# One inference step of a two-layer hybrid decoder on one core: the same operations in another order and on other engines

## The chip, the core and the metric

The kernel runs on one core of one Trainium2 chip. A core has a matrix engine (TensorE, PE in the profile; its weight loads are shown apart as PEld), three elementwise engines (VectorE = DVE, ScalarE = ACT, GpSimd = POOL) and SyncE (SP), which in this kernel issues every DMA. The metric is the time of the device in microseconds (us); lower is better.

## What is computed

There are 512 prompt tokens and 8 sequences with one new token each, handled together as T = 520 columns. Each of the two layers normalises x, multiplies by W_in, runs three mixers and adds the result of W_out to x:

```
h = rmsnorm(x) @ w_in                       # 1024 -> 3072 + 24 gates
A: GLU -> causal depthwise conv (31 taps) -> LayerNorm -> swish -> pointwise
B: trailing means over 2/4/8/16 tokens minus the token, one small product per group
C: attention, 8 query heads, 2 key/value heads: compressed blocks + selected
   blocks (top 8 of 64 rows) + window of 256, mixed by per-head sigmoid gates
x = x + concat(A * silu(zA), B * silu(zB), C * silu(zC)) @ w_out
```

The 8 sequences carry caches of 512 rows each; two of the three caches lie in pages that a page table names. New cache rows and states are outputs too.

## The kernel before, in words

The program is first written down as a list (class Plan): every engine instruction is an op, and ops that must stay together on one engine form a burst; an op alone or a burst is a *unit*. There are 3309 units, numbered as the program text makes them. `plan.place` then takes the units in the sequence of the string TUNE["order"], gives the buffers their slots in that sequence, and `emit` issues them so (line 352 is the one line that issues everything, which is why nearly every row of the profile has L352). Each engine runs its own units strictly in that sequence; across engines only data and buffers order them. A second string, TUNE["engines"], has one letter for each of the 756 elementwise ops that may run on one of several engines (v, s, g for VectorE, ScalarE, GpSimd). So the order on all five queues is written out by hand, number by number.

The large products are those of `product` (line 744): 1024 input rows in 8 chunks of 128 and 128 output columns; x and the weights are split in two fp32r parts each, and a chunk is one burst of 6 matmuls (high x high, high x low, low x high, for two halves of 260 tokens). `fetch` (592) loads the weights of one product as two halves of 256 KB, chunks 0-3 and 4-7, and `split` (724) makes the high and the low part of each half with two elementwise ops. A product holds two of the eight PSUM banks until `evac` (758) has read it.

`evac` multiplies by rb, the reciprocal norm of each token. `scale(c)` (765) makes the high and the low part of piece c of x and its square, and `sums` (689) adds the squares up by four small products in four 32-column strips of PE; `spread` (695) needs the sums of all 8 pieces, computes the reciprocal root by eleven ops on VectorE, stores it to a DRAM tile (rs) and loads it back broadcast (rb). So products can run before rb is there, but none can leave PSUM.

Small products come in several tile forms, told in the profile by rows * columns of the weights: 128\*128 (all large products and the transposes), 128\*64, 128\*32, 64\*128 (the attention scores), 64\*32 and 32\*32.

`constants` (625) also has 24 warm-up products (`warm`, 629-633), which give nothing that is used:

```
ve.memset(mean_w, 1.0 / 256.0)
warm = plan.bank("warm", "t")
for n in range(WARM // 2):
    with plan.burst():
        for k in range(2):
            te.matmul(warm[:, :128], mean_w, mean_w, start=True, stop=True)
```

Every fp32 product that is not a transpose is two matmul instructions on the chip, so the warm-up is 48 of them. `cmp_pages` (912) loads 32 pages of the compressed cache in a layer, each with a read of the page number first; `compress` (878) needs them. `decode` (1256) attends for the 8 sequences, in two groups of four.

Of the kernel before, what the change touches and what calls it, by code (L numbers as in the profile page):

```python
# [189 lines left out]
class Plan:  # L190
# [135 lines left out]
    def emit(self, tc, ctx):  # L326
# [60 lines left out]
        "vvvvgvvsssssvssgsvvggvggsvsvvssvvsgvvssvsvggsvvvgvgssgsggvvvgvsgsgsgvvggvvvsvvvvvssvsvsvsgggsvvvsvsgvgvsvgvgvssv"  # L387
        "vvsgsgsvssgvvsggsvgvsgsvsvggsvsggsvvggvggggvvssgvsssvsvsvggvvsgsgvggvvgvvgsssssggggssssvssssssvgvvggvvsvsvsgsgvv"
        "vsvvsvgsvvgvggssvvssvsvvvsvgvggggsgsvvgggggsvgvgvsssgvssvsssssvssssvsssgggvvvggsvgvvvvgvgsssssvvssvvsvvsgvvggsgg"
        "ggvggvvgvgsvvvvgsgsvvvsvgvsvsgvgsgsvsvsvsvggsvsgssggssvsvvvgvvgvgvggsvvsssvsvsssvssvgvvsssggggggvgvvvgsgsvvgssvg"  # L390
        "vsvgvsvvgsvssggvvsvgvvgvvggvsvvvvsvgvgvssvggsvvvsvssvgvsgvggvgsvggsgsgsgvgggvsggggvvvssgsvsvvsvsvsgggsgggvggvggs"
        "gsggssggssssvgsssvsvssvsgggsgvvsggvggvggvsggvssvsgvsgggssssvssvsvvvsssgvvggvggsgvvsssgggvgvgvsssssssssvsvvsvvsss"
        "sgvgvgvgvgvgvvvggvssvvvvssgvsvsvvsggvsgggvvsgsggvvsgsvgvsgggsggvsgggsgsgsvsvsvsvggvv"
    ),
    "order": (
# [1147 lines left out]
```

## Time and profile before

| | us |
|---|---|
| median of 3 runs | 624.89 (624.70 to 625.42) |
| the profiled execution, whole | 623.73 |
| its span, first to last instruction | 622.0 |

| engine | busy us | share of the span |
|---|---|---|
| PE | 606.4 | 97% |
| PEld | 536.7 | 86% |
| DVE | 433.7 | 70% |
| ACT | 259.7 | 42% |
| POOL | 226.2 | 36% |

Times in the views count from the first instruction of the span. In a list in order of time a row is: start, duration, engine, line, operation, out<-in, rows * columns of the weights and shape, and how many instructions were merged; in brackets the idle time before, and what ended it. Matmuls overlap, so the cost of a group is read from its start to the start of the next one, not from its duration.

### The profile page before, as it was taken

How to read it: one execution, taken by the hardware profiler on the slowest of the kernel's cores; microseconds unless marked ns; L12 is line 12 of the kernel's file. 1: busy time of each engine (PE TensorE's matmuls, PEld its weight loads, DVE VectorE, ACT ScalarE, POOL GpSimd, SP SyncE). 2: the span in 40 equal slices, each digit the busy share in tenths (PEclk: the TensorE clock that was granted, in tenths of full speed). 3: DMA queues.
4: the chain of work that ended last, by engine and by line, in shares of the span. 5: the costliest groups of instructions: out<-in, count | busy, mean ns of one | idle time of the engine just before them, and what ended most of it. 6: DMA issues, size and time to landing. Idle time of an engine off the chain costs nothing.

```text
span 622.0 us, 15002 instructions
## 1 busy us (share of the span) xinstructions
PE 606.4 (97%) x5526; PEld 536.7 (86%) x5526; DVE 433.7 (70%) x1222; ACT 259.7 (42%) x731; POOL 226.2 (36%) x250
## 2 busy tenths in 40 slices
PE   6999999999999999999999999999999999999997
PEld 5999998898868788579999999999985968677997
DVE  6535879966778697965465498887677678688221
ACT  4102125656683395431221132237575769543100
POOL 2123225442414363341522242556443535144700
PEclk9999999999999999999999999999999999999999
DMA  8755444322652346887546234342246135788622
GB/s 267 217 166 180 152 124 146 115 76 73 136 122 65 104 125 220 268 252 228 185 143 194 85 113 160 94 124 62 77 79 155 37 95 140 185 255 252 208 77 95
DMA packets 89130, 90.98 MB, mean 146 GB/s; under 512 B 25858, under 2 KB 59746, under 8 KB 88930
## 3 DMA queue, kind: packets, MB, share of 16 engines
q1 hardware_dynamic: 89058, 90.04, 48.9%
q8 instruction: 43, 0.70, 0.5%
q14 instruction: 29, 0.24, 0.1%
HBM read 75.32 MB, written 14.67 MB: 145 GB/s over the span
## 4 chain that ended last, share of the span: by engine, by line
PE 84%; DVE 6%; SPq 5%; DMA 3%; issue 2%; ACT 1%; ACTq 0%; DVEq 0%
PE banks L352 84%; DVE t L352 4%; SPq L352 3%; DVE small L352 2%; DMA t<-in_win 2%; SPq L616 1%; ACT t L352 1%; DMA t<-in_x 1%; DMA t<-in_cmp 0%; DVE keep L352 0%; ACTq L352 0%; DVEq L352 0%
## 5 line engine op out<-in xcount | busy, mean ns | idle before, releaser
L352 PE MATMUL banks<-t,t 128*128 128x260 f32 (+5 forms) x3960 | 490.0, 302 | 1.9 <-DVE t L352 0.8
L352 PEld LDWEIGHTS banks<-t,t 128*128 128x128 f32 (+3 forms) x3960 | 434.2, 178 | 32.8 <-issue 25.1
L352 POOL TENSOR_TENSOR t<-t,t 128x512 fp32r<-128x512 f32 (+4 forms) x84 | 111.4, 1332 | 129.2 <-PE banks L352 55.7
L352 ACT ACTIVATE t<-t 128x512 fp32r<-128x512 f32 (+4 forms) x130 | 78.5, 613 | 155.1 <-DVE t L352 56.8
L352 ACT ACTIVATE t<-t,small 128x384 f32<-128x384 f32 (+4 forms) x185 | 99.2, 552 | 16.2 <-DVE small L352 15.9
L352 PE MATMUL banks<-keep,t 128*128 128x128 f32 (+7 forms) x698 | 87.2, 311 | 1.9 <-DVE t L352 1.1
L352 DVE TENSOR_TENSOR t<-t,t 128x512 fp32r<-128x512 f32 (+3 forms) x92 | 71.0, 782 | 22.0 <-PE banks L352 16.0
L352 PEld LDWEIGHTS banks<-keep,t 128*128 128x128 f32 (+2 forms) x698 | 66.5, 161 | 22.1 <-issue 12.5
L352 DVE TENSOR_TENSOR t<-banks,t 128x520 f32<-128x520 f32 (+1 forms) x54 | 37.2, 693 | 63.8 <-PE banks L352 51.2
L352 DVE CUSTOM_DVE_ANT_0 t<-banks,keep,small 128x384 f32<-128x384 f32 (+3 forms) x128 | 64.3, 528 | 16.2 <-PE banks L352 16.0
L352 POOL TENSOR_SCALAR t<-t 128x512 fp32r<-128x512 f32 (+2 forms) x49 | 34.6, 707 | 88.3 <-PE banks L352 48.5
L352 ACT ACTIVATE t<-banks 128x512 f32<-128x512 f32 (+3 forms) x72 | 36.6, 525 | 62.1 <-PE banks L352 45.7
L352 PE MATMUL banks<-t,keep 128*32 128x130 f32 (+7 forms) x688 | 41.2, 306 | 6.7 <-DVE keep L352 4.8
L352 PEld LDWEIGHTS banks<-t,keep 128*32 128x32 f32 (+3 forms) x688 | 23.2, 116 | 20.5 <-DVE keep L352 5.0
L352 POOL TENSOR_SCALAR t<-t,small 128x384 f32<-128x384 f32 (+3 forms) x50 | 32.9, 671 | 21.2 <-DVE small L352 15.4
L352 ACT ACTIVATE small<-small 128x32 f32<-128x32 f32 (+3 forms) x76 | 23.5, 310 | 27.5 <-DVE small L352 27.4
L352 DVE COPY t<-banks 128x512 f32<-128x512 f32 (+2 forms) x37 | 21.5, 589 | 11.2 <-PE banks L352 7.3
L352 DVE SCALAR_TENSOR_TENSOR t<-t,t 128x520 f32<-128x520 f32 (+2 forms) x32 | 27.8, 873 | 1.3 <-ACT t L352 1.1
L352 POOL TENSOR_TENSOR t<-t,keep 128x520 f32<-128x520 f32 (+1 forms) x11 | 14.2, 1296 | 33.5 <-DVE t L352 20.4
L352 POOL TENSOR_TENSOR t<-t 128x520 f32<-128x520 f32 (+1 forms) x12 | 12.8, 1068 | 33.2 <-DVE t L352 13.9
L352 ACT ACTIVATION_READ_ACCUMULATOR t<-t,small 128x1 f32 x132 | 24.7, 187 | 0.0
L352 DVE SCALAR_TENSOR_TENSOR small<-small 128x130 f32<-128x130 f32 (+3 forms) x80 | 23.5, 296 | 1.5
(81 smaller groups left out, 358.1 us busy)
## 6 DMA issues: line engine op xcount, KB each, us to landing
t<-in_w_in SPq DMA_DIRECT2D x96, 256.0 KB
t<-in_cmp SPq DMA_DIRECT2D x64, 128.0 KB
t<-in_slc SPq DMA_DIRECT2D x64, 128.0 KB
t<-in_w_out SPq DMA_DIRECT2D x32, 256.0 KB
t<-in_x SPq DMA_DIRECT2D x16, 260.0 KB
t<-in_win SPq DMA_DIRECT2D x16, 256.0 KB
out_win<-t SPq DMA_DIRECT2D x16, 256.0 KB
t<-glu SPq DMA_DIRECT2D x12, 264.0 KB
```

The source lines that it names most:

```text
L352: fn(*[real(v) for v in o.a], **{k: real(v) for k, v in o.k.items()})
L616: pages[n] = tc.nc.sync.value_load(pt.real(plan)[0:1, n:n + 1], min_val=0, max_val=n_phys - 1)
```

## The change

Nothing is computed differently; the two strings are replaced. The letters go from v 274, s 251, g 231 to v 265, s 273, g 218. The order string is new in all its lines. The diff, cut to its beginning and end:

```diff
@@ -384,155 +384,155 @@
     "engines": (
-        "vvvvgvvsssssvssgsvvggvggsvsvvssvvsgvvssvsvggsvvvgvgssgsggvvvgvsgsgsgvvggvvvsvvvvvssvsvsvsgggsvvvsvsgvgvsvgvgvssv"
...
+        "sgvssssssgsgssssvgsvsvvvsvggvgsvvsgssvgvssggsvvvvgvsgvgvsgvvggvgsvssvsvgvvvsvgggvssvggvssgvgsvgvsvssgvvsvgvsvssg"
...
     ),
     "order": (
-        "78 16 35 0 36 15 27 33 17 79 2 3 4 18 34 37 80 19 39 81 84 22 40 5 6 21 115 38 82 43 57 47 20 44 48 7 41 85 59 "
-        "23 42 51 86 141 307 52 138 134 55 56 139 83 45 117 143 136 53 118 63 46 137 60 58 49 64 140 65 66 309 133 116 "
-        "145 67 68 69 87 121 8 369 61 50 144 310 54 70 9 122 119 25 10 123 71 88 72 11 73 308 74 75 311 142 76 120 124 62 "
...
-        "3270 3271 3016 3272 3285 3273 3238 3257 3286 3287 3239 3288 3289 3240 3274 3290 3291 "
+        "2 3 16 15 4 5 6 7 115 33 17 35 18 369 117 8 9 39 41 10 11 0 27 12 19 34 307 371 118 23 20 37 13 21 14 121 309 38 "
+        "36 79 40 51 47 45 22 122 78 43 144 49 42 123 372 308 55 46 375 142 61 376 377 310 50 348 378 63 313 80 124 53 82 "
+        "314 132 145 315 370 59 44 48 52 81 56 136 60 64 316 65 66 148 138 139 116 141 57 150 83 84 311 140 151 67 312 "
+        "373 54 85 58 68 86 69 87 70 221 71 119 374 317 120 72 73 74 318 88 75 76 89 25 90 319 549 379 143 77 133 380 137 "
+        "381 350 550 131 62 125 382 91 152 320 218 431 351 126 92 93 127 321 128 354 322 432 94 323 129 147 182 153 235 "
+        "383 183 355 324 154 237 95 134 356 435 433 184 96 97 325 98 326 99 327 349 216 434 155 100 101 436 149 102 437 "
...
+        "3272 3285 3238 3307 3286 3287 3273 2565 3288 3289 3239 3240 3290 3274 3308 3291 "
     ),
```

What the numbers say, read against the numbering of the units:

- Units 3 to 14 are the warm-up. Before, they stand in nine groups of 4 or 8 instructions among the first products and sums; after, all twelve stand ahead of everything else on PE. Unit 2, the memset that they read, is the first on VectorE after; before, it stood behind two ops on x.
- The first large product on PE before is k0 (units 84, ...) behind the sums of piece 0 and 8 instructions of warm-up; after, it is chunk 0 of v0 (121) directly behind the warm-up, then the sums of pieces 0 and 1. Then come 10 more chunks, out of v0, k2 and k1, then the sums of pieces 2 to 7 side by side, and then the rest of the four products k0, k1, k2, v0. All four are finished on PE before any other product begins (v1, 354 and on).
- On SP before: halves of k0, v0 and then page loads mixed with the second halves; after: x piece 0, then first halves of v0, k2 and k1 among the other pieces of x, both halves of k0, and the second half of k1 after the first page; the weights v1, q0 also stand ahead of most pages of the second group. The last of layer 0's compressed pages is the 63rd DMA before and the 71st after.
- On VectorE after, the first op on the finished sums (in `spread`) stands ahead of the low parts of k0 and k1's second halves and of pieces 5 and 6 of x.
- Changes of the tile form from one PE instruction to the next, counted along the two order strings: 186 before, 160 after.

## Rows read from the trace of the kernel before

**Rows 1.** the page: span, busy time of each engine, granted clock in 40 slices.

```profile
span 622.0 us, 15002 instructions
...
PE 606.4 (97%) x5526; PEld 536.7 (86%) x5526; DVE 433.7 (70%) x1222; ACT 259.7 (42%) x731; POOL 226.2 (36%) x250
...
PEclk9999999999999999999999999999999999999999
```

**Rows 2.** the chain in order of time: start, duration, what.

```profile
5.78 6.09 DMA t<-in_x
...
117.84 123.40 PE banks L352 x1126
...
276.82 259.20 PE banks L352 x2385
...
564.41 53.73 PE banks L352 x489
```

**Rows 3.** TensorE in order of time, the first 36 us.

```profile
4.82 0.66 PE L352 MATMUL banks<-t,keep 128*32 128x130 f32 x8 [4.82 <-DVE keep L352]
5.41 2.08 PE L352 MATMUL banks<-keep 128*128 128x128 f32 x8
7.14 1.94 PE L352 MATMUL banks<-t,t 128*128 128x260 f32 x6
9.02 0.66 PE L352 MATMUL banks<-t,keep 128*32 128x130 f32 x8
9.61 1.75 PE L352 MATMUL banks<-keep 128*128 128x128 f32 x8
11.28 0.65 PE L352 MATMUL banks<-t,keep 128*32 128x130 f32 x16
...
12.33 1.68 PE L352 MATMUL banks<-t,t 128*128 128x260 f32 x12
13.94 1.09 PE L352 MATMUL banks<-t,keep 128*32 128x130 f32 x32
...
16.50 1.05 PE L352 MATMUL banks<-keep 128*128 128x128 f32 x8
17.31 0.97 PE L352 MATMUL banks<-t,t 128*128 128x260 f32 x6
```

**Rows 4.** all engines in order of time, first 25 us; [idle before, what ended it].

```profile
0.74 1.28 ACT L352 ACT_TABLE_LOAD   x1 [0.74 <-PEq L1535]
...
3.35 0.63 ACT L352 ACTIVATE t<-t 128x512 fp32r<-128x512 f32 x1 [1.32 <-DMA t<-in_w_in]
...
4.03 0.70 DVE L352 TENSOR_TENSOR t<-t 128x520 f32<-128x520 f32 x1 [4.03 <-DMA t<-in_x]
...
5.11 0.17 DVE L352 MEMSET keep<- 128x128 f32 x1
...
23.02 0.66 SPq L352 DMA_DIRECT2D rs<-small  x1
```

**Rows 5.** busy time (and pieces) of PE, PEld, DVE, ACT, POOL; clock, DMA, by stretch.

```profile
22.00:34.00 12.00, 10.34 (x89) 9.86 (x88) 4.52 (x10) 2.54 (x4) 3.15 (x3) 1.00 0.74 232
34.00:50.00 16.00, 15.54 (x130) 15.36 (x128) 3.95 (x12) 0.00 (x0) 2.51 (x2) 1.00 0.47 143
```

**Rows 6.** who waited for whom: us in total, times, longest.

```profile
PEld banks L352 <- issue: 44.0, 131, 0.8
```

**Rows 7.** weight loads in order of time, 92 to 97 us.

```profile
95.04 0.25 PEld L352 LDWEIGHTS banks<-small 128*32 128x32 f32 x8
95.49 1.60 PEld L352 LDWEIGHTS banks<-t,t 128*128 128x128 f32 x13 [0.20 <-issue]
```

**Rows 8.** weight loads by form: names, operands, count, busy us, mean ns, idle.

```profile
L352 PEld LDWEIGHTS banks<-t,keep 128*32 128x32 f32 x512 | 12.9, 110 | 16.9 <-DVE keep L352 5.0 <-POOL t L352 3.3 <-issue 2.6
```

**Rows 9.** all engines in order of time, 22 to 36 us.

```profile
26.09 0.36 SPq L352 DMA_DIRECT2D t<-rs  x1
...
29.73 1.30 DVE L352 TENSOR_TENSOR t<-banks,t 128x520 f32<-128x520 f32 x2 [5.78 <-DMA t<-rs]
```

More of the change, by code (lines that the diff above doesn't have):

```diff
@@ L386 @@
     "engines": (
-        "vvvvgvvsssssvssgsvvggvggsvsvvssvvsgvvssvsvggsvvvgvgssgsggvvvgvsgsgsgvvggvvvsvvvvvssvsvsvsgggsvvvsvsgvgvsvgvgvssv"
[L388 to L393, printed above, removed]
+        "sgvssssssgsgssssvgsvsvvvsvggvgsvvsgssvgvssggsvvvvgvsgvgvsgvvggvgsvssvsvgvvvsvgggvssvggvssgvgsvgvsvssgvvsvgvsvssg"
+        "vgsvsvgvssvvgsggsvsvsvsgsgsvggsvsgvssgsvsgsssvsgsvssvsvvgggvvggvggggggvgggvvsgsvsssvgssvssssvsvgvsgvgvgvsvgvggvs"
+        "gvssgssggssgvvsssssssvssvssvgggsgsvssvggvvssvgssssvssgssssvssvvssssvsssgvgvvggvsvvgggggsvvsssvvvssssssvgggggvgvv"
+        "gsvgvvvvsgsvsvsgsvvvgvsgsvsggvsvvvvggggvgvsvgvsvgvgsggssssvvgggvgvvvvggssvsssvvgvvsgvgvsssgggsvgvvsvvvsvsvvgvggs"
+        "gsgvvsvvgggssgsvsvgvggsvgvgvvsvvgsgggsvssvvvsgsvggsgvgggvgsvsvvvvgvgsvsgvgsvgvssgggsvssgvvsvsvsvgggsgsgvvgvsgsgv"
+        "gssvsvssggsvssssssvsssssvvgsvvvvvvvvsgvvgvgsvvsgvvgvvgsssssssssvsvssssgggsggvgvgggvvvvsgsvvssssggsvsvsvvssvsvsss"
+        "ssggvvggvsvvggvgvsgssvvssvsvvsssssvgvsgsggvsvvgsgvgvggggsvsggvsgvvsgsvvvggsggvvvsvvg"
     ),
     "order": (
[140 rows of a table removed]
[140 rows of a table added]
     ),
```

269 rows, old and new, of the table TUNE are left out of this document.

## The prediction

> **What bounds the kernel now.** I read the page first, then the chain of waits, then TensorE's own list in order of time, and last the stretches in which TensorE has holes. [...] The chain confirms that PE sets the end and shows where it does so without a break [rows 2]: 123.40 us of nothing but PE from 117.84, and 259.20 us from 276.82. In these two stretches no other engine and no DMA matters, and an order can save there only what PE itself loses between two instructions. PE is without work for 622.0 - 606.4 = 15.6 us. Of these, 4.8 lie ahead of its first instruction [rows 3]. The list and the stretches of the first 50 us [rows 3, 5] show 12.00 - 10.34 = 1.66 and 16.00 - 15.54 = 0.46 more. Of the remaining 8.7, 3.9 are the tail, the last evacuation and its store (the last PE stretch of the chain ends at 564.41 + 53.73 = 618.1 [rows 2]); 4.8 are short waits, by the breaks in the chain mostly around the two decode steps.
>
> Busy is not the same as useful, though. The 48 warm-up instructions give nothing, and they are busy time. And the first needed product took far longer than the later ones. So the first 50 us hold more to be won than the holes show, and I price them apart.
>
> **Part 1: the start (warm-up first, x and four first halves first).** What PE spends before 50 us on anything but needed work at its later pace:
>
> - 4.82 until its first instruction.
> - The warm-up. Two groups of 8 take 7.14 - 5.41 = 1.73 and 11.28 - 9.61 = 1.67, 0.21 an instruction; a group of 8 later takes 17.31 - 16.50 = 0.81, 0.10 an instruction [rows 3]. With the other 32 at 0.10 this is 1.73 + 1.67 + 3.2 = 6.6.
> - The first chunk of k0 takes 9.02 - 7.14 = 1.88; two chunks later take 13.94 - 12.33 = 1.61, 0.80 each [rows 3]. Lost: 1.1.
> - Holes: 1.66 + 0.46 = 2.1 [rows 5].
>
> Together 14.6. After the change, the memset that the warm-up reads no longer stands behind an op on x (before: VectorE waited until 4.03 for x, and the memset came at 5.11); the other engines begin at 0.74 [rows 4], so I put the first warm-up instruction at 1.0. All 48 in a row: at 0.10 they take 4.9, at 0.21 they take 10.2. I take 20 at the slow pace, since in the run of before the pace was slow until about 11 us with holes between, and 28 at the fast one: 4.2 + 2.8 = 7.0. So the first needed product can start at 8.0. Are its operands there? A first half of weights was there 2.6 us after the first issue, at 3.35, and x at 4.03, issued after it [rows 4]; v0's half is now the third DMA, so I put it one transfer later than x had, near 5. The split (an op of 0.63 and one of 0.70) and x's two parts end near 6.5. That is before 8.0: the warm-up covers it. After that I allow 2.0 us of holes, as before. 8.0 + 2.0 = 10.0 against 14.6: **a gain of 4.6.** Bounds: with the fast pace and no hole 5.9 against 14.6, a gain of 8.7; with the slow pace and 5 us of holes 1.0 + 10.2 + 5.0 = 16.2, a loss of 1.6.
>
> The cover of the holes is thin, and it is the norm. Before, from the last sum of squares (13.94 + 1.09 = 15.0) VectorE's chain runs to the store at 23.02, the load back is issued at 26.09, and the first evacuation starts at 29.73 [rows 3, 4, 9]: 14.7 in all. After, eleven chunks (8.8) and two sums (0.5; 1.09 / 4 = 0.27 each) stand ahead of sums 2 to 7 (1.6): the last sum is at 8.0 + 10.9 = 18.9. Among the eleven ops of the chain VectorE now has five others instead of two, three more at 0.7, so the evacuation comes at 18.9 + 14.7 + 2.1 = 35.7. Until then PE can live on four products of 8 chunks, 25.6, and eight sums, 2.2: to 35.8. They just meet, with 0.1 us to spare. What sits ahead of the last sum is piece 7 of x: before, the eleventh large transfer landed at 5.78 + 6.09 = 11.87 [rows 2]; it now is the twelfth, one step of (11.87 - 3.35) / 10 = 0.85 later, 12.7. Behind it on ScalarE stand its scaling, its square and three more ops of about 0.7 before the square of piece 6, so the sums could run from 16.2; PE wants them at 17.3. On SP the store of rs stands ahead of the gate weights, and GpSimd waits for these before it makes the low parts of v1 and q0; rs would be stored at 18.9 + 8.0 + 2.1 = 29.0, the gate weights land some 3 us later, and v1's low part is there at 34, ahead of 35.8. I see nothing that must be late, and little that is early; that is what the 2.0 us of holes are for.
>
> **Part 2: tile forms side by side.** 26 of 186 changes of form go. What one costs: in the list of weight loads, eight loads of the 128\*32 form follow each other to 95.29, and the load of the 128\*128 form that follows starts at 95.49, 0.20 later, with nothing named that it waited for ("issue") [rows 7]. A load of that narrow form takes 0.11 itself [rows 8], which would be hidden in a run of one form; so about 0.1 is lost for good. The list of waits has 44.0 us of such "issue" in 131 pieces, 0.34 each [rows 6]; some of that lies under matmuls that still run. I take 0.1: 26 x 0.1 = **2.6**. Bounds: 0 (all hidden) and 26 x 0.34 = 8.8. [...]
>
> **Part 3: the letters and everything else.** 22 ops more for ScalarE (busy 259.7), 9 fewer for VectorE (433.7), 13 fewer for GpSimd (226.2) [rows 1]: some 0.7 us each, all on engines with at least 188 us to spare, hidden by the PE stretches of rows 2. If that cover were gone, it would show as new short waits. Before, the waits outside the start and the tail are 4.8; I leave them as they are: **0**, with bounds of -4.8 (all go) and +4.8 (they double). The loads of the pages end later in the queue (71st instead of 63rd DMA), at 2 us later by my count of issues; the second group of the compression also comes later on PE, so I cost this at nothing.
>
> **Sum.** 4.6 + 2.6 + 0 = 7.2. The profiled execution took 623.73 (span 622.0 and 1.7 around it): 616.5. The median of the runs is 1.16 above that execution, so I give 617.7.
>
> **The rivals.**
>
> *The norm comes too late (the other side).* The first op on the sums now stands on VectorE ahead of the low parts of k0, k1 and of pieces 5 and 6; it waits for the last sum, and while it waits nobody makes those parts. If piece 7 or a square is late, the sums, the low parts and rb are all late by the same amount, PE runs out of the four products, and banks cannot be freed. PE then stands from 35.8 on. It decides when rb comes more than 7.2 us after that, at 43 or later; at 46 the time is 617.7 + 10.2 = 627.9. For it: the in-order queues, the thin margin, the three more ops within the chain. Against it: piece 7 would have to land 7 us later than I count. Chance 0.14.
>
> *The start gives nothing.* The loads feed PE no faster than before, and only the forms pay: 624.9 - 2.6 = 622.3. For it: the DMA share in 22 to 34 us is 0.74 already [rows 5]. Against: the warm-up alone, moved into dead time, is worth more than this. Chance 0.10; half of that with the forms worth nothing as well, so 624.9.
>
> *The changes of form cost the whole wait.* 0.34 each: 4.6 + 8.8 = 13.4, 611.5. For it: the 44.0 us [rows 6]. Against: PE is 97% busy, so most of that wait lies under matmuls. Chance 0.12.
>
> *The warm-up is wasted.* Products just after a hole run at half pace, as the first chunk did (1.88 against 0.80 [rows 3]), although the page shows the upper level throughout. If PE stands between the warm-up and the first products, five chunks at 1.9 instead of 0.8 cost 5.5: 623.2. Against it: the operands are there at 6.5, before the warm-up ends. [...] No row of this run shows the granted clock fall. Chance 0.08.
>
> **How the numbers follow.** My forecast, 614 to 621.5, has 0.56; the rivals 0.14, 0.10, 0.12 and 0.08. The range of 8 in 10 leaves out the far part of the cheap end and the far part of the late norm: 611.0 to 624.5. A measurement here can tell about 0.2% (1.25 us) from no change. Slower by more: 0.14. Within 0.2%: 0.08, from the cases in which the start and forms both give little or the warm-up is wasted. Faster: 0.78.
>
> **What would show it right or wrong.** Right: warm-up instructions on PE from about 1 us on, the first 128x260 product near 8, no PE hole of over 1 us before 50, the first evacuation near 35.7 and PE not waiting for it; the sum of "issue" waits of PEld down by some 26 pieces; PE busy near 602, less than before by the forms and the slow chunk. Wrong: a hole on PE between 30 and 45 that ends with the load of rs or with an op of VectorE; a first product later than 11; decode waits grown by more than 3 us; a PE that stays as long as before from 117 us on, with the same price for each change of form.

## The result: 618.2 us, and the profile after

The changed kernel takes 618.23 us (median of 4 runs, 617.68 to 618.48) against 624.80 of the kernel before in the same session: ratio 0.9893, interval 0.9876 to 0.991. I had said 617.7, in a range of 611.0 to 624.5, with 0.78 for faster. The profiled execution took 618.43 against my 616.5 for it, so the gain between the two profiled executions is 5.3 us, where my sum was 7.2; between the medians it is 6.6.

The page of the kernel after, its lines that answer to [rows 1]: TensorE (PE) is idle for 616.7 - 605.0 = 11.7 us instead of 15.6, the granted clock reads 1.00 in all slices (what its record holds of the first microseconds stands in the last section). ScalarE has 22 instructions more, VectorE 9 and GpSimd 13 fewer.

```profile
span 616.7 us, 14975 instructions
...
PE 605.0 (98%) x5526; PEld 538.7 (87%) x5526; DVE 434.6 (70%) x1213; ACT 267.5 (43%) x753; POOL 212.1 (34%) x237
...
PEclk9999999999999999999999999999999999999999
```

PE in order of time, the first 36 us, answering to [rows 3] (start, duration, product, count; in brackets the idle time before and what ended it):

```profile
1.06 7.73 PE L352 MATMUL banks<-keep 128*128 128x128 f32 x48 [1.06 <-DVE keep L352]
8.55 0.96 PE L352 MATMUL banks<-t,t 128*128 128x260 f32 x6
...
17.40 1.54 PE L352 MATMUL banks<-t,keep 128*32 128x130 f32 x48
...
34.45 0.98 PE L352 MATMUL banks<-t,t 128*128 128x260 f32 x6 [0.24 <-DVE t L352]
```

The warm-up now fills dead time, the first needed chunk starts at 8.55 (I had said 8.0) and takes 0.96 instead of 1.94, the sums of squares end at 17.40 + 1.54 = 18.9 (said: 18.9), and no hole before 50 us is longer than 0.24. The memset that the warm-up reads stands at 0.84 instead of 5.11 [rows 4]. The end of the norm, VectorE in order of time, answering to [rows 9]: the first evacuation comes at 33.70, 2 us ahead of what I counted.

```profile
33.70 1.91 DVE L352 TENSOR_TENSOR t<-banks,t 128x520 f32<-128x520 f32 x3 [5.89 <-DMA t<-rs]
```

The same stretches as [rows 5], and the sum of "issue" waits of the weight loads that answers to [rows 6]:

```profile
22.00:34.00 12.00, 12.00 (x103) 12.00 (x101) 5.90 (x13) 0.00 (x0) 3.77 (x4) 1.00 0.55 154
34.00:50.00 16.00, 15.76 (x136) 15.01 (x135) 9.82 (x25) 3.75 (x6) 4.09 (x4) 1.00 0.69 214
```

```profile
PEld banks L352 <- issue: 33.3, 100, 0.9
```

Both stretches are now full (12.00 of 12.00, 15.76 of 16.00), and the issue waits fell by 10.7 us in 31 pieces. But the chain of waits, beside [rows 2], shows what else came in: in layer 1 the norm's store and load of rs stand in the chain. In the last decode stage the window's load does. That one is not new: it stood in the chain before, in a part that [rows 2] leaves out:

```profile
536.66 4.90 DMA t<-in_win
541.69 8.37 PE banks L352 x66
```

The kernel after:

```profile
108.90 148.56 PE banks L352 x1355
...
321.14 2.58 DMA rs<-small
323.80 5.95 DMA t<-rs
...
330.59 162.26 PE banks L352 x1549
...
532.82 3.97 DMA t<-in_win
```

In PE's list these are three holes that the kernel before did not have in this size (before, its longest after 50 us is 0.86, and its wait for the window at 541.69 is 0.65):

```profile
94.08 0.44 PE L352 MATMUL banks<-t,keep 128*32 128x136 f32 x8 [1.21 <-ACT t L352]
```

```profile
330.59 1.97 PE L352 MATMUL banks<-t,t 128*128 128x260 f32 x14 [1.29 <-DVE t L352]
```

```profile
536.17 1.07 PE L352 MATMUL banks<-t,keep 128*32 128x256 f32 x3 [1.10 <-DMA t<-in_win]
```

To see the balance I cut PE's time in each trace into pieces that add up: from the start of each instruction to the start of the next, with holes of over 0.15 us taken apart. Products of the decode stages are all that `decode` issues, its transposes too; narrow are the forms other than 128\*128.

| us | before | after | difference |
|---|---|---|---|
| ahead of the first instruction | 4.82 | 1.06 | -3.76 |
| warm-up | 6.58 | 7.49 | +0.91 |
| holes up to 50 us | 2.15 | 0.24 | -1.91 |
| holes after 50 us | 4.57 | 6.04 | +1.47 |
| narrow (tiled) products without the decode stages | 108.85 | 104.32 | -4.53 |
| full products and transposes | 469.96 | 469.37 | -0.59 |
| products of the decode stages | 20.92 | 24.03 | +3.11 |
| from the last start to the end | 4.11 | 4.11 | 0 |
| span | 621.96 | 616.66 | -5.30 |

The start gave 3.76 - 0.91 + 1.91 = 4.8, and 1.5 more that stand in the rows of products (the slow first chunk, 1.1, and the slow first sums, 0.4, both at the slow pace): 6.3 in all. The rest of these rows, 4.53 + 0.59 - 1.5 = 3.6, I put down to the forms; it is a remainder and no measurement, and it has in it, with the other sign, the transposes outside the decode stages, which take 1.5 longer. And 3.11 + 1.47 = 4.6 was given back in the decode stages and in new holes. By the middle of the kernel the lead was whole: the first sum of layer 1 starts at 319.33 before and at 312.59 after, 6.7 earlier, with as many instructions of PE ahead of it (2799 and 2803); the end is 5.3 earlier.

### The profile page after: what moved, and what is told of

Its sections match the earlier page's. It is cut to its first block, busy times and chain, and to the rows that moved or that the text cites. A ratio compares the mean times of both kernels' runs of the same rounds, so it can differ in the third digit from the quotient of the medians.

```text
span 616.7 us, 14975 instructions
## 1 busy us (share of the span) xinstructions
PE 605.0 (98%) x5526; PEld 538.7 (87%) x5526; DVE 434.6 (70%) x1213; ACT 267.5 (43%) x753; POOL 212.1 (34%) x237
## 4 chain that ended last, share of the span: by engine, by line
PE 84%; DVE 8%; DMA 5%; ACT 1%; issue 1%; SPq 1%; DVEq 0%; ACTq 0%
PE banks L352 84%; DVE t L352 5%; DVE small L352 2%; DMA t<-rs 2%; DMA out_pool_s<-small 1%; ACT t L352 1%; SPq L352 1%; DMA t<-in_cmp_w 1%; DMA t<-in_win 1%; DMA rs<-small 0%; ACT small L352 0%; DVE keep L352 0%; SPq L616 0%; DVEq L352 0%; ACTq L352 0%
## 5 line engine op out<-in xcount | busy, mean ns | idle before, releaser
L352 POOL TENSOR_TENSOR t<-t,t 128x512 fp32r<-128x512 f32 (+3 forms) x79 | 103.6, 1319 | 132.1 <-ACT t L352 33.9
L352 ACT ACTIVATE t<-t 128x512 fp32r<-128x512 f32 (+5 forms) x123 | 73.6, 612 | 161.5 <-DVE t L352 68.3
L352 PE MATMUL banks<-keep,t 128*128 128x128 f32 (+8 forms) x698 | 86.1, 311 | 1.1 <-DVE t L352 0.8
L352 DVE TENSOR_TENSOR t<-t,t 128x512 fp32r<-128x512 f32 (+5 forms) x97 | 70.1, 733 | 21.8 <-PE banks L352 8.0
L352 PEld LDWEIGHTS banks<-keep,t 64*128 64x128 f32 (+3 forms) x698 | 66.1, 161 | 21.3 <-issue 7.3
L352 POOL TENSOR_SCALAR t<-t 128x512 fp32r<-128x512 f32 (+3 forms) x57 | 38.3, 675 | 125.4 <-DMA t<-in_w_in 46.7
L352 DVE CUSTOM_DVE_ANT_0 t<-banks,keep,small 128x384 f32<-128x384 f32 (+3 forms) x128 | 64.2, 529 | 11.5 <-PE banks L352 10.7
L352 POOL TENSOR_TENSOR t<-t 128x520 f32<-128x520 f32 (+3 forms) x14 | 16.6, 1189 | 40.1 <-PE banks L352 21.1
L352 ACT ACTIVATE t<-t,keep 128x520 fp32r<-128x520 f32 (+2 forms) x21 | 17.0, 818 | 28.7 <-DVE t L352 26.0
L352 DVE CAST t<-t 128x512 fp32r<-128x512 f32 x32 | 17.9, 565 | 14.1 <-PE banks L352 10.2
L352 POOL TENSOR_SCALAR t<-t,small 128x384 f32<-128x384 f32 (+2 forms) x34 | 21.0, 626 | 19.2 <-DVE small L352 16.9
```

The source lines that it names most:

```text
L352: fn(*[real(v) for v in o.a], **{k: real(v) for k, v in o.k.items()})
```

## The experiments

Except for the letters, all kernels here are made the same way: the buffers keep the slots that the order string gives them, and a second string says in which order the units are issued. Units are named by their numbers. The edit common to all:

```diff
     plan.place([int(v) for v in tune["order"].split()])
+    plan.order = [plan.units[int(v)] for v in tune["then"].split()]
```

On the chips of these runs the kernel before takes 626.9 to 628.0 us (medians of 12 to 29 runs), so only ratios are compared. The changed kernel itself, run again on two of these chips:

> The changed kernel itself once more, beside the next three on one chip, so that they can be compared with it and not only with the kernel before. Both theories: ratio to the kernel before 0.989, as in its first runs (618.2 us on the first chip).

Measured 0.9906 (0.9876 to 0.9935).

> The changed kernel once more, beside the kernel with the waits covered, on the same chip: ratio to the kernel before 0.989 to 0.991 by both theories, holes near 1.3 to 2.7 at 331 us and 1.1 to 1.6 at 537 us.

Measured 0.9913 (0.9883 to 0.9944), with holes of 1.69 and 1.54. The gain is the same in all three sessions.

**The warm-up alone, in the kernel before.** Units 2 (memset) and 3 to 14 (48 instructions) go to the front of the issue order, nothing else:

```diff
-78 16 ... 17 79 2 3 4 18 34 ... 22 40 5 6 ...
+2 3 4 5 6 7 8 9 10 11 12 13 14 78 16 ... 17 79 18 34 ... 22 40 21 115 ...
```

> The kernel before, with one thing moved: the memset and all 48 warm-up instructions stand first on PE and VectorE; every other queue is untouched. My theory: the warm-up out of the way is worth nothing alone, because PE then only reaches sooner the wait for the norm (the hole that ended at 31.6 us), which stands where it stood: about 624.2, with that hole grown from 1.0 to some 3.5 us. Rival, the place of the warm-up is the gain: 624.8 - 5.7 = 619.1.

Measured 1.0007 (0.999 to 1.0025): nothing. PE starts at 1.06, but in the old order of loads the time turns into waits. I had expected one hole of some 3.5; there are several, for a weight's load and for a low part on GpSimd (1.67), and the holes behind PE's first instruction sum to 11.0 us against 6.7 in the trace of the kernel before.

```profile
1.06 8.21 PE L352 MATMUL banks<-keep 128*128 128x128 f32 x48 [1.06 <-DVE keep L352]
...
25.60 4.28 PE L352 MATMUL banks<-t,t 128*128 128x160 f32 x32 [0.83 <-DMA t<-in_w_in]
31.55 0.43 PE L352 MATMUL banks<-t,keep 128*32 128x130 f32 x8 [1.67 <-POOL t L352]
```

**The warm-up put back, in the kernel after.** Units 3 to 14 stand again between the first chunks:

```diff
-2 3 16 15 4 5 6 7 115 33 ... 369 117 8 9 39 41 10 11 0 27 12 19 34 ... 13 21 14 121 309 ...
+2 16 15 115 33 ... 369 117 39 41 0 27 19 34 ... 21 121 3 4 309 ... 40 5 6 51 ... 378 13 63 313 14 ...
```

> The changed kernel, with the 48 warm-up instructions put back between its first chunks (the memset stays first). My theory: they are on the path again. The first chunk starts at about 7.2 us, when its weights are split, 1.3 sooner, but 48 x 0.11 = 5.4 us of warm-up and about 2 us of slow pace fall on needed work: 618.2 - 1.3 + 7.4 = 624.3. Rival, the gain is made by the forms and the loads and not by the warm-up's place: 618.2.

Measured 0.9996 (0.9977 to 1.0014): the whole gain is gone, and the rival fell. PE starts at 6.53 at the slow pace (1.67 for a chunk), the sums start at 22.15 instead of 17.40, 4.8 later. In this execution the start is not all of the loss: the hole at layer 1's norm is 2.98 long instead of 1.29, and behind it, and behind one of 1.45 in the decode stage, the granted clock is 0.57 over 4 us.

```profile
6.53 1.67 PE L352 MATMUL banks<-t,t 128*128 128x260 f32 x6 [6.53 <-ACT t L352]
...
22.15 1.54 PE L352 MATMUL banks<-t,keep 128*32 128x130 f32 x48
```

By these two ratios neither half works alone: the early warm-up needs the new order of loads (without it: nothing), the new order needs the early warm-up (without it: nothing).

**No warm-up.** All 48 instructions left out (the products they warm up for stay):

```diff
-2 3 16 15 4 5 6 7 115 33 ...
+2 16 15 115 33 ...
```

> The kernel after without any of the 48 warm-up instructions; the rest in its order. The first needed product can then start when v0's low part is there, at 7.25 us. Theory (the slow pace is met by whatever PE runs first): some 18 instructions of the slow pace fall on needed products, each 0.1 to 0.12 us longer for 130 or 260 columns, so 2 us are lost against 0.9 won by the earlier start: 619.3 us, ratio 0.991, with a first chunk of over 1.5 us. Rival (the warm-up gives nothing, the products run at their later pace at once): 617.3, ratio 0.988, first chunk 0.96.

Measured 1.0006 (0.9981 to 1.0031), some 6 us worse than with it (0.9906 and 0.9913, on other chips); my 2 us were too little. The slow pace did fall on needed products: the first chunk starts at 6.94 and takes 1.67.

```profile
6.94 1.67 PE L352 MATMUL banks<-t,t 128*128 128x260 f32 x6 [6.94 <-ACT t L352]
```

The sums end at 20.1, 1.2 later than after. The rest came later: at layer 1's norm PE waited 3.98 us in the profiled execution (631.16 us, one of the longer ones, so its rows show the kind of loss and not its mean); in and behind that hole the granted clock fell to 0.50 (row by stretch: PE busy and pieces, granted clock, DMA share, GB/s). The other eleven executions have mean granted clocks of 0.988 to 0.997, those of the kernel before beside them 0.997 to 1.000, so such falls are in them too.

```profile
334.00:336.00 2.00, 0.00 (x0) 0.55 0.96 339
336.00:338.00 2.00, 1.77 (x8) 0.50 0.62 235
```

**Pages first.** Eleven of the first page loads go back ahead of k0's first weight half on SP:

```diff
-... 22 122 78 43 144 49 ... 46 375 142 61 ...
+... 22 122 144 142 145 136 148 138 139 141 150 140 151 78 43 49 ... 46 375 61 ...
```

> The kernel after with eleven of the first page loads put back ahead of k0's first weight half on SP, so that all weight halves behind them come later. Theory (the queue's order carries part of the start's gain): eleven issues of some 0.55 us each are 6 us by which the weights behind them come later; PE has holes of about that size before 30 us and the time is 624 us, ratio 0.9985. Rival (the loads have slack, the gain is the warm-up and x's pieces alone): 618.2, ratio 0.989.

Measured 1.0039 (1.0016 to 1.0063), 8 us worse than the kernel after (0.9906 in the same session). The issues took 12.3 us on SP, not 6, and the hole is as long as I said, 6.18; but behind it PE also ran at the lower clock until 30 us.

```profile
26.10 1.23 PE L352 MATMUL banks<-t,t 128*128 128x260 f32 x4 [6.18 <-DVE t L352]
```

```profile
26.10:30.00 3.90, 3.71 (x17) 3.41 (x18) 3.87 (x7) 0.00 (x0) 1.87 (x2) 0.56 0.81 273
30.00:34.00 4.00, 4.00 (x35) 4.00 (x35) 3.90 (x8) 0.63 (x1) 1.91 (x2) 1.00 0.03 8
```

**The forms undone, in the kernel after.** Thirteen full products go one place forward, between two narrow ones: 186 changes of form instead of 160.

```diff
-... 36 79 40 51 ... 45 22 122 78 43 ... 767 691 814 611 728 ...
+... 36 79 122 40 51 ... 45 22 78 43 ... 767 691 728 814 611 ...
```

> The kernel after with 13 wide products moved one place forward, each between two narrow products that stood side by side: 186 changes of form again instead of 160, everything else as it was, the start too. Theory (0.1 us a change, by the start-to-start times of the traces): 26 x 0.1 = 2.6 us more, 620.8 us, ratio 0.9935. Rival 1 (each change costs the whole issue wait of 0.34): 8.8 more, 627.0, ratio 1.003. Rival 2 (a change hides under other work): 618.2, ratio 0.989.

Measured 1.0011 (0.9988 to 1.0034) against 0.9906: 1.05%, 6.6 us, between theory and rival 1. The traces tell them apart. Both profiled executions (616.7 and 623.4) have the clock at 1.00; the holes grew from 6.28 to 8.04, so 6.78 - 1.76 = 5.0 us are left for 26 changes, 0.19 each. Against the kernel after on the same chip (620.4) it is 3.0 us, and more once that execution's own losses are taken out of it: 1.4 more of holes, 1.5 of clock (half of the 3 us that PE worked at a granted clock of 0.50), less 0.8 for 8 slow warm-up instructions fewer; 5.1, or 0.20 each. One of the thirteen places, 12 narrow and 24 full instructions, first in the kernel after, then here:

```profile
134.29 0.97 PE L352 MATMUL banks<-keep,t 64*128 64x256 f32 x12
135.19 3.14 PE L352 MATMUL banks<-t,t 128*128 128x260 f32 x24
138.26 0.40 PE L352 MATMUL banks<-keep,t 64*128 64x288 f32 x2
```

```profile
135.96 0.62 PE L352 MATMUL banks<-keep,t 64*128 64x256 f32 x6
136.51 0.98 PE L352 MATMUL banks<-t,t 128*128 128x260 f32 x6
137.41 0.62 PE L352 MATMUL banks<-keep,t 64*128 64x256 f32 x6
137.96 2.42 PE L352 MATMUL banks<-t,t 128*128 128x260 f32 x18
140.31 0.40 PE L352 MATMUL banks<-keep,t 64*128 64x288 f32 x2
```

After: 138.26 - 134.29 = 3.97. Undone: 140.31 - 135.96 = 4.35 for the same instructions, 0.38 for two changes. Six narrow instructions take 0.55 alone (136.51 - 135.96), twelve in a row 0.90 (135.19 - 134.29): six more cost 0.35, so 0.20 goes with the change. The starts of the single instructions in the two traces show where it goes. Not one step is long at a change, but two, and they are the same in both runs: into the narrow form 0.22 and, to its second pair, 0.22, then 0.11 to 0.12 a pair; out of it 0.20 to 0.21 and then 0.22, then 0.12. Over the 30 places after 40 us of the kernel after where PE goes from a narrow form into at least four full instructions without a hole, the medians are 0.22, 0.225 and 0.12. The 0.1 that I had read from [rows 7] (over all changes after 40 us, PE's step across one is 0.09 longer into a narrow form, 0.11 out of it) is the first of the two long steps; the second costs as much again here. Into the forms of 32 columns the second step is longer by less (0.135 instead of 0.11 for products of 128 columns), so the price depends on the form.

**The forms apart, further.** As before, but 45 full products, 250 changes:

```diff
-... 236 551 552 384 ... 108 234 444 163 ...
+... 236 551 444 552 384 ... 108 234 163 ...
```

> The changed kernel, with 45 chunks of large products moved between neighbours of one narrow form: 250 changes of tile form instead of 160, nothing else moved. At 0.1 us a change: 618.2 + 9.0 = 627.2. Rival one, changes are hidden: 618.2. Rival two, each costs the whole 0.34 us of an issue wait: 618.2 + 30.6 = 648.8.

Measured 1.0378 (1.0353 to 1.0404), 30 us more than the kernel after, which would be 0.33 a change, about the price of rival two. The trace says otherwise: of 649.0 - 616.7 = 32.3 us, 9.6 are new holes (15.87 against 6.28), and the lower clock while PE worked costs 5.6 (a mean clock of 0.989 is 6.8, of which 1.3 lie in those holes); 17.1 are left, 0.19 a change. The largest hole and what follows it:

```profile
348.68 1.67 PE L352 MATMUL banks<-t,t 128*128 128x260 f32 x6 [4.88 <-DVE t L352]
```

```profile
349.00:352.00 3.00, 3.00 (x14) 0.50 0.43 156
```

**The forms together, in the kernel before.** Thirteen groups moved next to their like: 170 changes instead of 186.

```diff
-35 0 36 15 27 ... 84 22 40 5 ...
+35 0 15 27 ... 84 22 36 40 5 ...
```

> The kernel before, with 13 narrow groups moved next to one of their form: 170 changes of form instead of 186, nothing else moved. At 0.1 us a change: 624.8 - 1.6 = 623.2. Hidden: 624.8. At 0.34: 619.4.

Measured 1.0019 (1.0003 to 1.0035). This decides nothing: at 33.6 and 544.0 PE has holes of 3.3 us, both with a lower granted clock behind them (0.60 from 34 to 38, 0.50 from 544 to 548), which swallow the 1.6 to 3 us in question. Whether the moves made them is open. The second:

```profile
543.96 1.08 PE L352 MATMUL banks<-t,keep 128*32 128x256 f32 x8 [3.35 <-DMA t<-in_win]
```

**The old letters, in the kernel after.** The order stays, the engines string is that of before. This changes the engine of 416 of the 756 operations; the totals differ by 22, 9 and 13 only.

```diff
-    "engines": (   # s 273, v 265, g 218
+    "engines": (   # s 251, v 274, g 231: the string of the kernel before
```

> The kernel after, its order kept, with the engine letters of the kernel before (ScalarE 22 operations fewer, VectorE 9 and GpSimd 13 more). It asks where the gain of the forms went: the steps of the two decode stages take some 5 us longer on PE after than before. Theory 1 (the letters cost nothing, the order alone made those waits): 618.2 us, ratio 0.989, decode waits as after. Theory 2 (the letters made them): 614, ratio 0.983. Rival (the new letters are needed by the new order, VectorE too late with its 9 more): 621 to 624, ratio 0.995, new holes ended by VectorE.

Measured 1.079 (1.0746 to 1.0835): 676.7 us, far outside both theories and the rival, whose sign (holes ended by VectorE) it shows. PE has 40 us of holes, most of them ended by VectorE, and the mean clock is 0.975. The first is in the first product:

```profile
14.24 1.96 PE L352 MATMUL banks<-t,t 128*128 128x260 f32 x14 [2.58 <-DVE t L352]
```

```profile
PE banks L352 <- DVE t L352: 19.9, 17, 3.4
PE banks L352 <- DVE small L352: 10.0, 8, 3.0
```

**Norm early, warm-up shorter.** 36 warm-up instructions (units 12 to 14 left out); in layer 1 the norm's last operations (1710 to 1713) ahead of three low parts (two of x, one of a weight), its store (1714) ahead of two weight loads:

```diff
-... 1704 1687 1699 1705 1680 ... 1863 1692 1825 1762 1710 1910 1711 ...
+... 1704 1687 1705 1680 ... 1863 1710 1711 1712 1713 1714 1699 1692 1825 ...
```

> The kernel after with two edits: 36 warm-up instructions instead of 48, and in layer 1 the norm's last ops on VectorE ahead of two low parts, its store ahead of two weight loads on SP. Theory: v0's low part is there at 7.24 us and the first needed product started at 8.55, so 12 warm-up instructions less (12 x 0.112) give 1.3; the load of rs in layer 1 comes 1.4 us earlier and the hole of 1.29 at 330 us goes. Together 2.6: 615.6 us, ratio 0.985, with a first needed product at 7.25 and no hole over 0.3 before the first evacuation of layer 1. Rival 1 (the low parts moved back are needed at once, and the holes come back elsewhere): only the start's part, 616.9, ratio 0.987. Rival 2 (the slow pace at the start lasts for a time, not for a count of instructions, and falls on needed products instead): 618.2, ratio 0.989.

Measured 0.991 (0.988 to 0.994), the same as the kernel after beside it (0.9906). Each part did its work: the first needed chunk at 7.36 instead of 7.79, the load of rs issued at 322.75 instead of 324.12. But the load took until 329.7, the hole shrank only from 2.65 to 1.56, and a pair of holes in the decode stage (1.48 and 0.49) had the clock at 0.57 behind it; it fell behind the hole of 1.73 that ends at 93.97 too (mean of this execution 0.993, of the kernel after 1.000). The slow pace was over before the first needed product (22 of the 36 warm-up instructions are slow), so it did not fall on needed work.

```profile
538.00:542.00 4.00, 4.00 (x22) 0.57 0.85 226
```

**The waits covered.** As the last, and: the two weight loads (2008, 2069) and a small store behind the load of rs; transposes (2915) and a full product (2938) ahead of the decode product that waits for the window (3017).

```diff
-... 1713 1727 2008 2069 1696 1714 1313 ... 1729 1715 1766 ... 2932 3017 3027 ... 3018 2915 ... 2971 2938 ...
+... 1727 1696 ... 1729 1715 2008 2069 1313 1766 ... 2932 2915 2938 3017 3027 ... 3018 ... 2971 ...
```

> The kernel after with three edits against the waits that its trace showed. Start: 36 warm-up instructions instead of 48. Norm of layer 1: its last operations ahead of two low parts on VectorE, its store and load ahead of two weight loads and a small store on SP. Second decode stage: TensorE runs a group of transposes and a wide product ahead of the product that waits for the window's load. [...] Rival (the holes only move to the next wait, as when the norm alone was moved): ratio 0.989 to 0.991, with a hole of over 1 us somewhere behind them.

The forecast was some 0.8 at the start, 1.3 to 3 at the norm and 1.1 to 2 in the decode stage, a ratio of 0.981 to 0.985, with no hole of over 0.6 at 330 or 536 us. In it the long holes count twice, for a lower clock behind them; that was my estimate, and no run shows a length from which it holds: the clock fell behind a hole of 1.45 and not behind one of 3.09. Measured 0.987 (0.9838 to 0.9903), between it and the rival: 619.5 us against 621.82 of the kernel after beside it (0.9913): the fastest of all, 8.5 us under the kernel before on that chip. Over the kernel after it gains 2.3 us by the medians, but the two intervals overlap, so this step is likely and not settled. The hole at the norm is gone, the clock is 1.00 in all slices; the decode hole became two, 0.91 and 0.95, near the rival's hole of over 1.

```profile
321.70 9.10 PE L352 MATMUL banks<-t,t 128*128 128x260 f32 x72
330.73 0.43 PE L352 MATMUL banks<-t,keep 128*32 128x130 f32 x8
```

```profile
535.57 1.16 PE L352 MATMUL banks<-t,keep 128*32 128x256 f32 x3 [0.91 <-DMA t<-in_win]
...
538.88 0.66 PE L352 MATMUL banks<-keep,t 128*128 128x128 f32 x4 [0.95 <-DVE t L352]
```

## Why the prediction was right, and where not

**Part 1, the start: right in kind, too low.** Said 4.6, measured 6.3. The times on which it rests came as said: warm-up from 1.06 (1.0), 20 instructions at the slow pace, 48 in 7.5 (7.0), first chunk at 8.55 (8.0), last sum at 18.9 (18.9; here two misses cancel, a start 0.55 later and chunks of 0.74 instead of 0.80). The 2.0 us of holes that I had allowed were 0.24, and that is nearly the whole difference. The cover that I called thin held: the store of rs was issued at 26.83, 7.9 us after the last sum, where I had put 10.1, and the first evacuation came at 33.70 and not at 35.7. What I had not seen is how much the halves need each other: I wrote that the warm-up alone, moved into dead time, is worth more than nothing, and by itself it is worth nothing (1.0007).

**Part 2, the forms: too low.** Said 2.6 at 0.1 a change; by the balance 3.6, 0.14 each; by undoing them and by parting more 0.19 to 0.20, which would be some 5.0 for 26. (The 1.4 between them is about what the transposes lost in the same rows of the balance.) I had read one long step in the list of weight loads and taken it for the whole; there are two. The lower bound of 0 was wrong: the step across a change is 0.09 to 0.11 longer by the medians, and the next one is longer too (0.225 instead of 0.12 on the way out of a narrow form).

**Part 3, letters and the rest: the step that failed.** I had put 0, and 4.6 us were lost there, nearly the bound of +4.8: 3.1 in the decode stages, 1.5 in holes. The step is "I leave them as they are" for the short waits, which had no row behind it: the load of rs in layer 1, which was covered before, ended PE's work for 1.29, and the window's load for 1.10 instead of 0.65; a third wait, for ScalarE at 94.08, took 1.21. My own sign of being wrong, decode waits grown by more than 3 us, came about with the 3.1. That these waits can be bought back in part, the last experiment makes likely. The letters I read by their totals (22, 9, 13) and priced "22 ops more"; in truth 416 operations change their engine, and with the old letters the new order takes 55 us more (1.079 - 0.991, of 627 us), so letters and order are one plan. Whether the letters have a part in the 4.6 us is not shown: the old order with the new letters was not run. The products of 512 columns in the decode stages took 5.1 us before; after, they and those of 256 columns take:

```profile
L352 PE MATMUL banks<-t,keep 128*32 128x512 f32 x32 | 6.6, 598 | 0.2 <-DVE t L352 0.2
...
L352 PE MATMUL banks<-t,keep 128*32 128x256 f32 x32 | 4.3, 391 | 1.1 <-DMA t<-in_win 1.1
```

(3.2 and 0.8 of idle before for those of 256.) They wait too, inside their groups, while another product of the group still runs and no hole shows. Eight instructions of 512 columns take 1.00 from first start to next product where nothing holds them; the other groups took 1.32 and 1.55 before, 1.54, 1.70 and 2.12 after. In two of the three after, a later weight load of the group is released by the load of a page of the cache for the selected blocks (in_slc), at 244.34 and 562.54; in the groups of 256 columns by window loads at 251.86 and 536.79. How much of the 3.1 us these loads make stays open.

So the predicted time was hit by errors that cancel, which is luck: 1.7 and 1.0 too little at the gains, 4.6 too little at the losses; 4.6 + 2.6 = 7.2 said, 6.3 + 3.6 - 4.6 = 5.3 measured. And the median came nearer (0.5 off) than the profiled execution (1.9 off), because I had put it 1.16 above that execution and it fell 0.20 below. PE's busy time, said to be near 602, is 605.0.

**The rivals.** The late norm did not come in layer 0, but it came in layer 1, of the same kind and 1.29 us long. That the start gives nothing fell with the first chunk at 8.55 and the holes up to 50 us. The whole wait of 0.34 fell: two runs put a change at 0.19 to 0.20, and the 0.33 of the run with the forms apart is change, holes and clock together. The wasted warm-up fell here, but its price was seen in the run with the pages first (granted clock 0.56 from 26.1 to 30); its reading that the first chunk of the kernel before stood behind a hole was wrong, for that chunk followed warm-up instructions that were slow themselves. The trace of the kernel before shows no fall of the granted clock (1.00 in its record from 10.87 to 621.85 us); the changed kernel run again, with a hole of 2.65 (ended by VectorE, which had waited for the load of rs), has the granted clock at 0.50 behind it, but a hole of 3.09 in the run with the pages first left it at 1.00.

## What to carry to other kernels

A reordering is one plan: the early warm-up without the new loads (1.0007), and the new order without the early warm-up (0.9996) or without its choice of engines (1.079), were worth nothing or less here, so price it by what arrives last at each place, not by sums of busy time; and count operations that change their engine, not the totals. Then look for the new waits: a gain that PE makes early is a demand on every later load to be early too, and part of it is lost at the first two or three that are not (holes of 1.21, 1.29 and 1.10 us here); look for such waits inside the products' own durations too, where no hole shows (3.1 us in the decode stages here). Part narrow products of one form only where something else is gained by it: here the step behind the change was as long as the one across it (medians of 0.225 and 0.22 instead of 0.12), so the pair cost twice what a single row showed (0.19 to 0.20 instead of 0.1).

## What had not been expected of the hardware

Some holes cost more than their length, for the granted clock was lower behind them. Holes of 1.29 (the kernel after), 1.56 (norm early) and 1.69 (the kernel after, run again) at layer 1's norm left it at 1.00; behind one of 2.65 (the other time that the kernel after was run again) it was at 0.50, the lower of the two values in the clock's record of the kernels before and after (1.00 and 0.50), until past 334, and PE has 9 pieces of work in 2 us instead of 19:

```profile
330.00:332.00 2.00, 0.01 (x1) 0.90 1.03 357
332.00:334.00 2.00, 2.00 (x9) 0.50 0.63 238
334.00:336.00 2.00, 2.00 (x18) 0.75 0.04 8
336.00:338.00 2.00, 2.00 (x19) 1.00 0.00 0
```

Behind holes of 2.02 (forms apart, 0.91 in the mean from 80 to 120), 2.98 (the warm-up put back, 0.57 over 4 us), 3.32 and 3.35 (forms together, 0.60 and 0.50 over 4 us), 3.98 (no warm-up, 0.50 from 336 to 340), 4.88 (forms apart, 0.50 from 349 to 352) and 6.18 (pages first, 0.56 from 26.1 to 30) the clock was lower as well. No limit is read from these, for the length alone does not decide. Behind a hole of 3.09 that ended at 341.42 in the run with the pages first it stayed at 1.00:

```profile
342.00:344.00 2.00, 2.00 (x22) 1.66 (x21) 0.19 (x1) 0.00 (x0) 1.20 (x3) 1.00 0.40 144
```

Behind one of 1.23 in the same run it was at 0.57 from 548 to 552, and behind 1.45 (the warm-up put back, 0.57 over 4 us) and 1.73 (norm early, 0.993 in the mean of the execution) it fell too; behind 1.54 (the kernel after, run again, 0.999 in the mean) it did not. A pair of 1.48 and 0.49 had a fall behind it (norm early, 0.57 from 538 to 542), another of 1.25 and 0.67 had none (the forms undone, 1.00 from 538 to 546).

The slow pace at the start cannot be read from the column of the granted clock. It says 1.00 while warm-up instructions come every 0.21 us instead of 0.11, but the trace's record of the clock has no entry yet. Its first entry, at the upper level (1.00), stands at 5.51 us in the kernel after and at 10.87 in the kernel before, just where the slow instructions end (the last of them start at 5.28 and 10.62); without the warm-up it stands at 13.34, and the products are slow until there (the 60 instructions from 9.57 on take 9.12; the same in the kernel after, 7.44). So the 1.00 ahead of it, on the pages of both kernels too, is no reading. That the slow pace is the lower level (0.50) is likely, at twice the time an instruction, but no entry shows it. And the slow pace does not end at a fixed instruction: of 48, 20 were slow in the first trace, 13 and 22 in the two later ones of the same kernel; the first needed chunk started at 8.55, 7.79 and 8.70, so a start can come out some 0.8 us earlier or later by this alone.
